# Scaling of a head half's outputs, moved from the step of their squares into the step after it

## The chip, the cores and the metric

The kernel runs on one core of one Trainium2 chip. The metric is the device time of one execution in microseconds (us). It is one layer of a gated mixer block over 2048 tokens of width 1024, in float32 with matrix products split into a high and a low part.

## What is computed

The reference, cut to the part that the change touches (the other branch, the norms at both ends and the output projection are left out):

```python
def _hgrn2_chunk_step(state, inp):          # scan over chunks of 64 tokens, per head
    ...
    o = o_inter + jnp.einsum('bhts,bhsv->bhtv', scores, v)
    ...

def reference(x, c, w_ada, ...):
    h = rms_norm(x, g_pre[l]) * (1.0 + scale) + shift
    (pv, pg, hq, hf, hi, hg, mg_pool, mg_hgrn) = jnp.split(h @ w_in[l], split_idx, axis=-1)
    ...
    o = hgrn2(q, k, v, logf)                                   # 8 heads of 128
    o = rms_norm(o, hgrn_norm_g[l]).astype(x.dtype).reshape(b, s, HGRN_WIDTH)
    branch_b = (o * jax.nn.silu(hg)) @ w_hgrn_o[l]
    merged = jax.nn.sigmoid(mg_pool) * branch_a + jax.nn.sigmoid(mg_hgrn) * branch_b
    y = merged @ w_out[l]
    x = x + gate * rms_norm(y, g_post[l])
```

The change is in the `rms_norm(o, ...)` of each head: the mean of the squares of a token's 128 outputs, its power -1/2, and the product of the outputs with it.

## The kernel before

The 2048 tokens are worked through in two passes of 1024 (`p` 0 and 1), and a pass in two halves of 512 tokens (`t` 0 and 1). A pass has these stages: the value projection for all heads (`v_job`); a loop over the 8 heads; the pool branch's output projection (`a_job`, accumulators psA), the recurrent branch's output projection and the merge (`b_job`, psB), and the last projection (`y_job`, psy). Pass 0 loads raw weights from memory, splits each on ScalarE (a cast, L172) and VectorE (a subtraction, L172) into a tile `whl` and stores the split tiles; pass 1 loads the split tiles back.

In the head loop three projections are made for a head by `quad`: "fq", and then "m" and "gp" (head 7 has "gp" first). A quad makes seven products of 12 matmuls each by a Strassen-like scheme, in four PSUM banks pa, pb, pe and pd. The sixth product (into pe) and the seventh (into pd) matter here: pd is first filled by ScalarE with a copy of pa, `A.copy(d, a)` at L496 (in the profile `pdm<-pam` or `pdgp<-pagp`), and TensorE then adds the seventh product to it. So TensorE can't begin the seventh product before that copy is done. The copy reads what the fifth product left in pa, so it could run while TensorE makes the sixth.

Between the products, `quad` calls `tick()`, which advances every active generator by one step (up to its next `yield`). The recurrence of a head is such a generator, `hgrn(p, h, t, cx)`, two of them per head, one for each half `t`; they are advanced one after the other in the same tick. They start after the head's "fq" quad and end in the next head's middle quad. Their last steps are: the output matmuls `po` (one PSUM bank of four 128x128 blocks), then four Squares on ScalarE (L687, `junk`), each with its sum into a column of `ss`; two small instructions on GpSimd (POOL in the profile) that turn the sums into the factor (L688 and the power, L390, 128x4); four scalings on ScalarE (L692, `on<-po,ss`); later four transposes on TensorE (L698, `pot<-ident,on`), and VectorE's product with norm gain and gate (L700, `sgg`), which is split into Gh and Gl for the stage psB. The outputs of heads 0 to 6 are scaled while the next head's middle quad runs ("m"; in head 7 "gp"), just ahead of its copy at L496; those of head 7 during `a_job`.

The order of the instructions within a step is not that of the code alone: the framework's scheduler merges the steps and the quad's own work into one order for each engine, and each engine then works strictly in that order, waiting on semaphores. What shares ScalarE's order with the scalings is the quad's copies, the weight casts, and the next head's score preparation (copies L605, L608, L638 into tiles `X8` and `X32`, and L709, a copy of 16 columns for the pool branch).

Of the kernel before, what the change touches and what calls it, by code (L numbers as in the profile page):

```python
# [69 lines left out]
def tile_block(ctx: ExitStack, tc: tile.TileContext, x, c, w_ada, b_ada, g_pre, g_post, w_in,  # L70
# [20 lines left out]
    def utile(name, dt=F32):  # L91
        return up.tile([P, T], dt, tag="u", name=name)
# [296 lines left out]
    def tt(o, a, b, op=MUL, e=None):  # L389
        return (e or V).tensor_tensor(o, a, b, op=op)  # L390
# [131 lines left out]
    def hgrn(p, h, t, cx):  # L522
# [164 lines left out]
            A.activation(junk[:, 0:P], po[:, cc, :], AF.Square, accum_out=ss[:, cc:cc + 1])  # L687
        G.tensor_scalar(ss, ss, 1.0 / P, EPS, op0=MUL, op1=ADD)  # L688
        tt(ss, ss, mh[:, 0:NT], op=ALU.pow, e=G)
        on = utile("on" + n)  # L690
        for cc in range(NT):
            A.activation(on[:, cc * P:(cc + 1) * P], po[:, cc, :], AF.Copy, scale=ss[:, cc:cc + 1])  # L692
        yield
        yield
        yield
        pot = px.tile([P, T], F32, tag="px", name="pot" + n)
# [308 lines left out]
    for p in range(NPASS):  # L1005
# [34 lines left out]
        for h in range(NH):  # L1040
# [22 lines left out]

            quad("fq" + n, cx, fq, tick)
            active.extend(hgrn(p, h, t, cx) for t in range(2))
            tick()
            for i, kind in enumerate(KINDS[h == NH - 1]):
# [67 lines left out]
```

## Time and profile before

| | |
|---|---|
| median of 3 runs | 1851.86 us (1851.43, 1851.86, 1857.75) |
| profiled execution, its own time | 1851.48 us |
| its span in the profile | 1849.7 us |
| granted TensorE clock, mean of the span | 0.997 of full speed |
| TensorE busy (PE) | 1782.6 us, 96% |
| weight loads (PEld) | 1456.7 us, 79% |
| VectorE busy (DVE) | 1089.1 us, 59% |
| ScalarE busy (ACT) | 799.9 us, 43% |
| GpSimd busy (POOL) | 80.0 us, 4% |

The span is the time from the first to the last recorded instruction; the execution's own time is 1.8 us more. A share is an average over all stages. In rows of instructions the time is counted from the span's start, and what stands in brackets is how long the engine sat idle before the instruction and what ended that wait.

### The profile page before, as it was taken

The page shows a single profiled execution, that of the slowest core. Times are in us where ns is not written, and L with a number is a line of the kernel's source. Part 1 is how long each engine was busy: PE and PEld are TensorE (multiplying, and loading weights), DVE is VectorE, ACT ScalarE, POOL GpSimd, SP SyncE. Part 2 cuts the span into 40 slices and gives each one's busy share as a digit, 9 for nine tenths or more (in the row PEclk, how much of TensorE's full clock was granted, in tenths as well). Part 3 has the DMA queues.
Part 4 walks back from the last instruction along what each step waited for, and adds up shares of the span by engine and source line. Part 5 has one row for each costly group of instructions (what it writes and reads, how often), then busy time and mean ns, then how long its engine had stood idle before and what let it go on. Part 6 is the DMA issues. An engine that isn't in the chain of part 4 may idle for free.

```text
span 1849.7 us, 31713 instructions
## 1 busy us (share of the span) xinstructions
PE 1782.6 (96%) x12053; PEld 1456.7 (79%) x12053; DVE 1089.1 (59%) x2328; ACT 799.9 (43%) x1863; POOL 80.0 (4%) x136
## 2 busy tenths in 40 slices
PE   5999999999999999999999999999999999999997
PEld 4788878878888777787788778878888788788886
DVE  7568877887888884565432255465455456533322
ACT  4746656656556562223322335445344344311111
POOL 1100000000000000000000000000000000000000
PEclk9999999999999999999999999999999999999999
DMA  8697676676767759987887765664764764694476
GB/s 298 233 322 277 221 268 243 231 261 225 266 241 246 247 201 320 361 288 255 295 310 242 246 193 175 224 206 154 234 205 159 231 201 162 233 340 163 141 258 230
DMA packets 236530, 444.19 MB, mean 240 GB/s; under 512 B 18989, under 2 KB 109786, under 8 KB 236378
## 3 DMA queue, kind: packets, MB, share of 16 engines
q1 hardware_dynamic: 236378, 442.17, 69.9%
q8 instruction: 95, 1.56, 0.3%
q14 instruction: 57, 0.47, 0.1%
HBM read 269.61 MB, written 172.49 MB: 239 GB/s over the span
## 4 chain that ended last, share of the span: by engine, by line
PE 79%; ACT 6%; DMA 3%; DVE 3%; POOL 2%; issue 2%; SPq 1%; POOLq 0%; DVEq 0%; ACTq 0%
PE psB L278 9%; PE psV L278 8%; PE psy L278 8%; PE pafq L278 6%; PE pagp L278 6%; PE pam L278 5%; PE pefq L278 5%; PE psA L278 4%; PE pegp L278 4%; PE pem L278 3%; PE psa L278 3%; PE pbfq L278 2%; PE pbm L278 2%; PE pdfq L278 2%; PE pdm L278 2%; PE pbgp L278 2%
## 5 line engine op out<-in xcount | busy, mean ns | idle before, releaser
L172 DVE TENSOR_TENSOR whl<-wr,whl 128x512 fp32r<-128x512 f32 x210 | 143.7, 689 | 83.6 <-ACT whl L172 82.6
L172 ACT CAST whl<-wr 128x512 fp32r<-128x512 f32 x210 | 129.8, 620 | 128.6 <-DMA wr<-in_w_hgrn_o_dram 22.4
L278 PE MATMUL psy<-whl,mgh 128*128 128x512 f32 x512 | 160.1, 393 | 1.4 <-DVE y L390 0.7
L278 PE MATMUL psV<-whl,hB 128*128 128x512 f32 x512 | 161.3, 397 | 0.1
L278 PE MATMUL psB<-Gh,whl 128*128 128x512 f32 x512 | 158.6, 390 | 0.0
L578 DVE COPY_PREDICATED PT<-mask,psa 128x256 f32<-128x256 uint8 x160 | 86.1, 548 | 51.5 <-PE psa L278 51.5
L278 PEld LDWEIGHTS psy<-whl,mgh 128*128 128x128 f32 x512 | 95.0, 188 | 22.5 <-DMA whl<-scr_y 1.7
L278 PEld LDWEIGHTS psB<-Gh,whl 128*128 128x128 f32 x512 | 96.1, 188 | 20.5 <-issue 0.5
L278 PEld LDWEIGHTS psV<-whl,hB 128*128 128x128 f32 x512 | 96.6, 191 | 19.8 <-ACT V L787 0.3
L278 PE MATMUL psV<-whl,lB 128*128 128x512 f32 x256 | 100.8, 395 | 0.0
L278 PE MATMUL psB<-Gl,whl 128*128 128x512 f32 x256 | 100.0, 391 | 0.0
L278 PE MATMUL psy<-whl,mgl 128*128 128x512 f32 x256 | 100.0, 391 | 0.0
L278 PE MATMUL pam<-hT,whl 128*128 128x512 f32 x256 | 87.2, 402 | 0.0
L278 PE MATMUL pagp<-hT,whl 128*128 128x512 f32 x256 | 86.1, 397 | 0.0
L278 PE MATMUL psA<-Ph,whl 128*128 128x512 f32 x256 | 82.6, 397 | 3.4 <-DVE sm L390 1.7
L278 PE MATMUL pafq<-hT,whl 128*128 128x512 f32 x256 | 84.0, 389 | 0.0
L390 DVE TENSOR_TENSOR K<-K,TT 128x256 f32<-128x256 f32 x192 | 81.2, 424 | 1.0 <-PE psa L278 0.9
L278 PEld LDWEIGHTS psa<-X,K 128*32 128x32 f32 x2816 | 50.1, 110 | 29.8 <-issue 21.1
L172 ACT CAST mgh<-sm 128x512 fp32r<-128x512 f32 x32 | 19.7, 620 | 121.3 <-DVE sm L390 121.3
L390 DVE TENSOR_TENSOR y<-psy,gg 128x512 f32<-128x512 f32 x32 | 21.9, 688 | 73.9 <-ACT jy L893 73.7
L278 PE MATMUL psa<-X,K 128*32 128x48 f32 (+2 forms) x2816 | 61.0, 208 | 2.1 <-DVE PT L572 2.1
L572 DVE COPY_PREDICATED PT<-mask,psa 128x256 f32<-128x256 uint8 (+1 forms) x96 | 51.9, 541 | 18.3 <-PE psa L278 18.3
(358 smaller groups left out, 4307.5 us busy)
## 6 DMA issues: line engine op xcount, KB each, us to landing
wr<-in_w_in_dram SPq DMA_DIRECT2D x122, 256.0 KB, 4.4
whl<-scr_y SPq DMA_DIRECT2D x48, 512.0 KB, 4.4
sm<-Sd SPq DMA_DIRECT2D x64, 256.0 KB, 4.3
whl<-scr_v SPq DMA_DIRECT2D x32, 512.0 KB, 3.4
wa<-in_w_ada_dram SPq DMA_DIRECT2D x32, 256.0 KB, 5.4
x<-in_x_dram SPq DMA_DIRECT2D x32, 256.0 KB, 5.5
Vd<-V SPq DMA_DIRECT2D x32, 256.0 KB, 2.4
scr_v<-whl SPq DMA_DIRECT2D x16, 512.0 KB, 2.8
```

Source lines behind the costliest of these rows:

```text
L172: return A.copy(hi, src32), V.tensor_tensor(lo, src32, hi.bitcast(F32), op=SUB)
L278: PE.matmul(o, lhsT=l, rhs=r, start=start, stop=stop, skip_group_check=True)
L390: return (e or V).tensor_tensor(o, a, b, op=op)
L572: V.copy_predicated(dst.rearrange("p (c a) b -> p c a b", c=NT), m.unsqueeze(1).broadcast_to(shp), src.unsqueeze(2).broadcast_to(shp))
L578: V.copy_predicated(dst.rearrange("p (c q) a b -> p c q a b", c=NT), m, src.rearrange("p c (a b) -> p c a b", b=b).unsqueeze(2) .broadcast ...
```

## The change

One `yield` moves up by a few lines, ahead of the scalings; the number of steps stays the same. The scalings (L692 before, L693 after) now belong to the step after the Squares, and both halves' Squares are made in the tick before.

```diff
             A.activation(junk[:, 0:P], po[:, cc, :], AF.Square, accum_out=ss[:, cc:cc + 1])
         G.tensor_scalar(ss, ss, 1.0 / P, EPS, op0=MUL, op1=ADD)
         tt(ss, ss, mh[:, 0:NT], op=ALU.pow, e=G)
+        yield
         on = utile("on" + n)
         for cc in range(NT):
             A.activation(on[:, cc * P:(cc + 1) * P], po[:, cc, :], AF.Copy, scale=ss[:, cc:cc + 1])
-        yield
         yield
         yield
         pot = px.tile([P, T], F32, tag="px", name="pot" + n)
```

No instruction is added or removed; the scheduler puts some in another place. In the names below the numbers after a tile's name are pass, head and half, and a buffer number.

The first place is ScalarE in pass 0 during head 1's "m" quad, where head 0's outputs are scaled, up to the copy at L496 (`pdm`). Before:

```order
L687 ACTIVATE junk0_0_0_1_2461,ss0_0_1_2460<-po0_0_1_2450 128x128
L692 ACTIVATE on0_0_0_2445<-po0_0_0_2424,ss0_0_0_2434 128x128 x4
L687 ACTIVATE junk1_0_0_1_2463,ss0_0_1_2460<-po0_0_1_2450 128x128
L608 COPY X8_0_1_0_2686<-sq0_1_0_2273 128x16x16
L687 ACTIVATE junk2_0_0_1_2465,ss0_0_1_2460<-po0_0_1_2450 128x128
L605 COPY X8_0_1_1_2713<-sq0_1_1_2186 128x16x16
L687 ACTIVATE junk3_0_0_1_2467,ss0_0_1_2460<-po0_0_1_2450 128x128
L692 ACTIVATE on0_0_1_2471<-po0_0_1_2450,ss0_0_1_2460 128x128 x4
L496 COPY pdm0_1_2526<-pam0_1_2304 128x512
```

Now:

```order
L687 ACTIVATE junk0_0_0_1_2456,ss0_0_1_2455<-po0_0_1_2445 128x128
L693 ACTIVATE on0_0_0_2546<-po0_0_0_2424,ss0_0_0_2434 128x128
L687 ACTIVATE junk1_0_0_1_2458,ss0_0_1_2455<-po0_0_1_2445 128x128
L693 ACTIVATE on0_0_0_2546<-po0_0_0_2424,ss0_0_0_2434 128x128
L687 ACTIVATE junk2_0_0_1_2460,ss0_0_1_2455<-po0_0_1_2445 128x128
L693 ACTIVATE on0_0_0_2546<-po0_0_0_2424,ss0_0_0_2434 128x128
L687 ACTIVATE junk3_0_0_1_2462,ss0_0_1_2455<-po0_0_1_2445 128x128
L693 ACTIVATE on0_0_0_2546<-po0_0_0_2424,ss0_0_0_2434 128x128
L608 COPY X8_0_1_0_2686<-sq0_1_0_2273 128x16x16
L693 ACTIVATE on0_0_1_2551<-po0_0_1_2445,ss0_0_1_2455 128x128 x4
L605 COPY X8_0_1_1_2713<-sq0_1_1_2186 128x16x16
L496 COPY pdm0_1_2516<-pam0_1_2304 128x512
```

The four scalings of half 0 are now dealt out between the Squares of half 1, and the two copies into X8, which stood between those Squares, stand behind them; one of them is now behind the scalings of half 1. The copy `pdm` still comes last. Heads 2 to 6 of pass 0 read the same way, with the L709 copy also moved behind half 1's scalings in heads 2, 4 and 6. In pass 1 all four scalings of half 0 alternate with all four Squares of half 1; L605 stands just ahead of half 1's scalings, and behind them come L638 and L608 in heads 1, 3 and 5 (before: L638 between the Squares, L608 behind `pdm`), L709 and L608 in heads 2, 4 and 6 (before: L709 between the Squares, L608 where it is now).

The second place is ScalarE in pass 0 during head 7's "gp" quad, where head 6's outputs are scaled. Before:

```order
L687 ACTIVATE junk0_0_6_1_7534,ss0_6_1_7533<-po0_6_1_7523 128x128
L692 ACTIVATE on0_6_0_7518<-po0_6_0_7497,ss0_6_0_7507 128x128 x4
L687 ACTIVATE junk1_0_6_1_7536,ss0_6_1_7533<-po0_6_1_7523 128x128
L605 COPY X8_0_7_1_7793<-sq0_7_1_7254 128x16x16
L687 ACTIVATE junk2_0_6_1_7538,ss0_6_1_7533<-po0_6_1_7523 128x128
L687 ACTIVATE junk3_0_6_1_7540,ss0_6_1_7533<-po0_6_1_7523 128x128
L692 ACTIVATE on0_6_1_7544<-po0_6_1_7523,ss0_6_1_7533 128x128 x4
L496 COPY pdgp0_7_7599<-pagp0_7_7372 128x512
L172 CAST whl194_7632<-wr193s1_7630 128x512
L608 COPY X8_0_7_0_7766<-sq0_7_0_7341 128x16x16
L750 ACTIVATE sgg0_7_1_7627<-c22gp0_7_7411 128x512
```

Now:

```order
L687 ACTIVATE junk0_0_6_1_7529,ss0_6_1_7528<-po0_6_1_7518 128x128
L605 COPY X8_0_7_1_7793<-sq0_7_1_7254 128x16x16
L687 ACTIVATE junk1_0_6_1_7531,ss0_6_1_7528<-po0_6_1_7518 128x128
L687 ACTIVATE junk2_0_6_1_7533,ss0_6_1_7528<-po0_6_1_7518 128x128
L687 ACTIVATE junk3_0_6_1_7535,ss0_6_1_7528<-po0_6_1_7518 128x128
L496 COPY pdgp0_7_7589<-pagp0_7_7372 128x512
L172 CAST whl194_7632<-wr193s1_7630 128x512
L608 COPY X8_0_7_0_7766<-sq0_7_0_7341 128x16x16
L750 ACTIVATE sgg0_7_1_7617<-c22gp0_7_7411 128x512
L693 ACTIVATE on0_6_0_7620<-po0_6_0_7497,ss0_6_0_7507 128x128 x4
L693 ACTIVATE on0_6_1_7625<-po0_6_1_7518,ss0_6_1_7528 128x128 x4
```

Here both scalings move behind the copy `pdgp` and the three instructions that follow it. In pass 1 head 7's "gp" quad reads the same, with L638 between the Squares and L608 ahead of `pdgp`.

The third place is TensorE in `a_job` of pass 0, where head 7's scaled outputs are transposed (pot). Before:

```order
L278 MATMUL psA0_6_0_8418<-Ph0_3_0_7493,whl206_8196 128x512
L698 MATMUL pot0_7_0_8432<-ident_87,on0_7_0_8321 128x128 x4
L278 MATMUL psA0_6_1_8452<-Ph0_0_1_7842,whl206_8196 128x512
L278 MATMUL psA0_6_1_8452<-Pl0_0_1_7843,whl206_8196 128x512
L278 MATMUL psA0_6_1_8452<-Ph0_0_1_7842,whl206_8196 128x512
L698 MATMUL pot0_7_1_8442<-ident_87,on0_7_1_8347 128x128 x4
L278 MATMUL psA0_6_1_8452<-Ph0_1_1_7874,whl206_8196 128x512
```

Now:

```order
L278 MATMUL psA0_7_0_8485<-Pl0_3_0_7494,whl207_8263 128x512
L698 MATMUL pot0_7_0_8432<-ident_87,on0_7_0_8375 128x128 x4
L278 MATMUL psA0_7_0_8485<-Ph0_3_0_7493,whl207_8263 128x512
L278 MATMUL psA0_7_1_8499<-Ph0_0_1_7842,whl207_8263 128x512
L278 MATMUL psA0_7_1_8499<-Pl0_0_1_7843,whl207_8263 128x512
L698 MATMUL pot0_7_1_8442<-ident_87,on0_7_1_8380 128x128 x4
L278 MATMUL psA0_7_1_8499<-Ph0_0_1_7842,whl207_8263 128x512
```

Both groups of transposes now stand 23 matmuls later, in the next accumulator pair. In pass 1 they move by 7 and 10 matmuls, within the same pair. On ScalarE, head 7's eight Squares now all come ahead of its eight scalings, in both passes. GpSimd's order is unchanged; SyncE's and VectorE's change by a few neighbouring rows around these places.

## Rows read from the trace of the kernel before

**Rows 1.** The head of the profile's page: the span, and each engine's busy time in us (share of the span) and instructions.

```profile
span 1849.7 us, 31713 instructions
PE 1782.6 (96%) x12053; PEld 1456.7 (79%) x12053; DVE 1089.1 (59%) x2328; ACT 799.9 (43%) x1863; POOL 80.0 (4%) x136
```

**Rows 2.** Who waited for whom, TensorE alone: engine, tile and line that waited, what it waited for, us in total, times, longest.

```profile
PE pdm L278 <- ACT pdm L496: 14.4, 12, 1.3
...
PE pdgp L278 <- ACT pdgp L496: 3.2, 2, 2.1
PE pot L698 <- ACT on L692: 2.2, 1, 2.2
```

**Rows 3.** The same for ScalarE: its wait for GpSimd's factor.

```profile
ACT on L692 <- POOL ss L390: 47.3, 32, 2.2
```

**Rows 4.** TensorE in order of time: start, duration, the instruction, and in brackets its idle time before it. The first matmul of the seventh product in pass 0's head 1, in pass 0's head 7 and pass 1's head 7, and the second group of head 7's transposes in pass 0.

```profile
239.89 0.50 PE L278 MATMUL pdm<-hT,whl 128*128 128x512 f32 x1 [1.24 <-ACT pdm L496]
...
677.83 0.50 PE L278 MATMUL pdgp<-hT,whl 128*128 128x512 f32 x1 [2.15 <-ACT pdgp L496]
...
755.33 0.66 PE L698 MATMUL pot<-ident,on 128*128 128x128 f32 x4 [2.19 <-ACT on L692]
...
1583.24 0.50 PE L278 MATMUL pdgp<-hT,whl 128*128 128x512 f32 x1 [1.06 <-ACT pdgp L496]
```

**Rows 5.** ScalarE in order of time in pass 0's head 1, from the scalings of head 0's half 0 to the copy pdm.

```profile
234.06 1.14 ACT L692 ACTIVATE on<-po,ss 128x128 f32<-128x128 f32 x4 [1.41 <-POOL ss L390]
235.07 0.29 ACT L687 ACTIVATE junk<-po 128x128 bf16<-128x128 f32 x1
...
235.32 0.43 ACT L608 COPY X<-sq 128x256 f32<-128x256 f32 x1
235.62 0.31 ACT L687 ACTIVATE junk<-po 128x128 bf16<-128x128 f32 x1
...
235.88 0.44 ACT L605 COPY X<-sq 128x256 f32<-128x256 f32 x1
236.17 0.32 ACT L687 ACTIVATE junk<-po 128x128 bf16<-128x128 f32 x1
236.34 0.24 ACT L687 ACTIVATION_READ_ACCUMULATOR junk<-po 128x1 f32 x1
238.20 1.14 ACT L692 ACTIVATE on<-po,ss 128x128 f32<-128x128 f32 x4 [1.62 <-POOL ss L390]
239.22 0.61 ACT L496 COPY pdm<-pam 128x512 f32<-128x512 f32 x1
```

**Rows 6.** ScalarE at the same place in pass 0's head 2.

```profile
306.81 1.15 ACT L692 ACTIVATE on<-po,ss 128x128 f32<-128x128 f32 x4 [1.41 <-POOL ss L390]
...
309.10 0.25 ACT L687 ACTIVATION_READ_ACCUMULATOR junk<-po 128x1 f32 x1
309.19 0.25 ACT L709 COPY PV<-halo 128x16 f32<-128x16 f32 x1
310.98 1.14 ACT L692 ACTIVATE on<-po,ss 128x128 f32<-128x128 f32 x4 [1.54 <-POOL ss L390]
312.00 0.61 ACT L496 COPY pdm<-pam 128x512 f32<-128x512 f32 x1
```

**Rows 7.** ScalarE at the same place in pass 1's head 1.

```profile
1142.54 1.14 ACT L692 ACTIVATE on<-po,ss 128x128 f32<-128x128 f32 x4 [1.42 <-POOL ss L390]
...
1145.28 0.19 ACT L687 ACTIVATION_READ_ACCUMULATOR junk<-po 128x1 f32 x1
1147.17 1.14 ACT L692 ACTIVATE on<-po,ss 128x128 f32<-128x128 f32 x4 [1.70 <-POOL ss L390]
1148.18 0.61 ACT L496 COPY pdm<-pam 128x512 f32<-128x512 f32 x1
```

**Rows 8.** ScalarE at the same place in pass 1's head 2.

```profile
1213.97 1.14 ACT L692 ACTIVATE on<-po,ss 128x128 f32<-128x128 f32 x4 [1.41 <-POOL ss L390]
...
1216.55 0.19 ACT L687 ACTIVATION_READ_ACCUMULATOR junk<-po 128x1 f32 x1
1218.34 1.15 ACT L692 ACTIVATE on<-po,ss 128x128 f32<-128x128 f32 x4 [1.60 <-POOL ss L390]
...
1219.66 0.61 ACT L496 COPY pdm<-pam 128x512 f32<-128x512 f32 x1
```

**Rows 9.** GpSimd in order of time: the first of the pair of instructions that make the factor, for half 0 and half 1 of head 0 and for half 1 of head 6, all in pass 0.

```profile
232.33 0.53 POOL L688 TENSOR_SCALAR ss<-ss 128x4 f32<-128x4 f32 x1 [32.03 <-ACT junk L687]
...
236.68 0.22 POOL L688 TENSOR_SCALAR ss<-ss 128x4 f32<-128x4 f32 x1 [2.65 <-ACT junk L687]
...
674.03 0.99 POOL L688 TENSOR_SCALAR ss<-ss 128x4 f32<-128x4 f32 x1 [2.49 <-ACT junk L687]
```

**Rows 10.** VectorE in order of time: what it ran when the first and the third of these ran (a sum or difference of two 128x512 tiles).

```profile
232.13 0.68 DVE L239 TENSOR_TENSOR wr<-wr67s,wr 128x512 f32<-128x512 f32 x1
...
674.29 0.67 DVE L239 TENSOR_TENSOR wr<-wr193s,wr 128x512 f32<-128x512 f32 x1
```

**Rows 11.** TensorE in order of time: the last matmul of the fifth product (into pagp) in pass 0's head 7.

```profile
672.58 0.39 PE L278 MATMUL pagp<-hT,whl 128*128 128x512 f32 x1
```

**Rows 12.** Busy time by stretch: us, then busy us (instructions) of PE, PEld, DVE, ACT and POOL, granted clock, share of the DMA engines, GB/s. The stretch of a_job in pass 0, and that of psB behind it.

```profile
710.00:763.00 53.00, 48.11 (x271) 40.05 (x265) 20.90 (x39) 14.89 (x48) 3.28 (x6) 1.00 0.97 345
763.00:850.00 87.00, 87.00 (x382) 71.28 (x381) 53.24 (x81) 18.50 (x31) 0.41 (x2) 1.00 0.83 287
```

## The prediction

> **What bounds the kernel now.** I read the page's head first: TensorE is busy 96% of the span, ScalarE 43%, GpSimd 4% [rows 1]. So an edit on ScalarE pays only where TensorE stands still for it. The view of who waited for whom, for TensorE alone, says where: 12 times for the copy pdm (14.4 us), twice for the copy pdgp (3.2 us), once for head 7's scalings (2.2 us) [rows 2]. That is 19.8 us, all that this edit can remove from TensorE directly. The same view for ScalarE says what makes those copies late: ScalarE waited 32 times for GpSimd's factor, 47.3 us in all, 1.5 us each [rows 3]. The timelines show the order of events: scalings of half 0, three Squares of half 1, a wait of 1.62 us for the factor, scalings of half 1, and only then the copy at L496 [rows 5], for which TensorE has by then waited [rows 4].
>
> **What the change does to each place.** No instruction is added or removed, so only waits and order can pay. I take the time t0 at which half 0's first scaling starts as fixed, since everything ahead of it is as before (in pass 1 one Square moves, dealt with below), and ask when the copy at L496 starts.
>
> Pitches from rows: four scalings take 1.01 us until the next Square starts, 0.25 each; a Square followed by other work takes 0.25, a copy into X8 0.30; a Square's start to the end of its readout is 0.41 (236.17 to 236.58); four scalings until the copy is 1.02 [rows 5].
>
> Pass 0, heads 1, 3, 5. Before: last readout ends at t0+2.52, the second scaling starts 1.62 later, pdm at t0+5.16 [rows 5]. Now three scalings and two Squares precede the last Square: 3 x 0.25 + 2 x 0.25 = 1.26, readout ends at 1.67. With the same 1.62 the scalings start at 3.29, and 1.02 + 0.30 for the one X8 copy now behind them puts pdm at 4.61: 0.55 us earlier. The fourth scaling and the other X8 copy (0.55) fit into the 1.62 of waiting, so they cost nothing; without that wait they would cost themselves.
>
> Pass 0, heads 2, 4, 6. Before: readout ends at t0+2.54, pdm at 5.19, and the wait from readout to scaling is 1.63 [rows 6]. Now 1.67 + 1.63 + 1.02 + 0.30 and some 0.2 for the L709 copy, which also moved behind: 4.82, 0.37 earlier.
>
> Pass 1, heads 1, 3, 5. Before: readout at t0+2.93, wait 1.70, pdm at 5.64 [rows 7]. Now four scalings and three Squares precede: 4 x 0.25 + 3 x 0.25 + 0.41 = 2.17; then 1.70 + 1.02, and two X copies (0.60) that now stand ahead of pdm: 5.49, 0.15 earlier. L608 waits for a VectorE step behind L605; L605 ends more than 2 us before L608's turn, so I count no wait.
>
> Pass 1, heads 2, 4, 6. Before: readout 2.77, wait 1.60, pdm 5.69 [rows 8]. Now 2.17 + 1.60 + 1.02 + 0.30 + 0.2 = 5.29, 0.40 earlier.
>
> Each of these gains is smaller than the wait it cuts into (1.24 in the row, 1.2 on average) [rows 2, 4], so it counts in full: 3 x (0.55 + 0.37 + 0.15 + 0.40) = 4.4 us.
>
> Head 7's "gp" quad. Both scalings leave the way of pdgp altogether. The copy can start when the fifth product ends, about 672.97 in pass 0 [rows 11], and takes 0.6; TensorE needs it at 677.83 - 2.15 = 675.68. So the full waits of 2.15 and 1.06 go [rows 4]. What is late next: the scalings wait for VectorE's sum behind pdgp, but their transposes come only after the seventh product, 2.7 us on. 3.2 us.
>
> Head 7's transposes in pass 0. They waited 2.19 us [rows 4]. At 0.23 us a matmul, 23 matmuls further on is 5.3 us after the place they should have had (753.14), that is 758.4, when the scalings, which ended before 755.33 even in the old order, have long been done. 2.19 us. The outputs reach psB later by 3 us, which needs them only with the last quarter of its first 48 matmuls, over 7 us after it starts; I count nothing. Pass 1 had no wait there and gets none.
>
> Sum: 4.4 + 3.2 + 2.2 = 9.8 us.
>
> **GpSimd against VectorE.** The 1.62 us are not a constant. GpSimd's first instruction takes 0.22 us in one row, 0.53 and 0.99 in others [rows 9], and both long ones ran beside a VectorE addition of two 128x512 tiles [rows 10]. The half 1 pair now starts 0.85 us sooner in pass 0, when VectorE is still at the previous scores. Its bounds are 0.22, as now (nothing lost), and 0.53, the nearest long row (0.31 lost in each of six heads, 1.9 us). VectorE's step there is half as long as that addition and partly reads PSUM, so I stay near the lower bound: 0.1 each, 0.6 us.
>
> The Trainium skill ("GPSIMD Engine Reference", section 1, Specifications) has GpSimd share its SBUF interfaces with VectorE, with contention when VectorE reads two SBUF inputs. The trace agrees, with the 0.53 and 0.99 above; by the rule alone, taken at 0.53, the sum would be 7.9, and without it 9.8.
>
> So the forecast is 9.2 us off the profiled execution's own time of 1851.48 (its span and 1.8 us around it): 1842.3. The median of the runs is 0.38 above that execution, so **1842.7** on the median's scale, 0.5% below it. About 0.5%, 9.3 us, is what a measurement of this kernel can tell from no change, so the forecast lies on the bound.
>
> **Rivals.**
>
> *The gain is waited out in a_job.* There the DMA engines are 0.97 busy at 345 GB/s and TensorE 48.11 of 53 us [rows 12]. If transfers set the pace there, what pass 0 gained before it (3 x 0.92 + 2.15 - 0.6 = 4.3) and the transposes' 2.19 come back as waits for tiles. Left: 9.2 - 6.5 = 2.7, or 1849.2. For it: that share. Against: those loads are issued as earlier work releases them, so they start earlier too, and psB behind it is busy 87.00 of 87 us [rows 12], with no sign of starving.
>
> *GpSimd's factor takes its long time everywhere.* At 0.99 in place of 0.22, 0.77 more in each of twelve heads 1 to 6: 9.2 us, of which 0.6 are already counted. Left: about 0.6, or 1851.2. Against: the one long row is from head 7's quad; the long one of head 0 is 0.53 [rows 9]. (It is what the rule above would give at its worst.)
>
> *Scalings and Squares don't overlap* (slower). No row shows a scaling that starts right behind a Square. If each waited for the other's end, a scaling would be 1.14 - 3 x 0.25 = 0.38 and a Square with its readout 0.41 [rows 5], 0.83 a pair with two small gaps, in place of 0.5 to 0.55. For a pair cost c the twelve heads together gain 3 x [(2.52 - 3c - 0.30) + (2.54 - 3c - 0.5) + (2.93 - 4c - 0.60) + (2.77 - 4c - 0.2)] = 27.5 - 42c, and 5.4 us come from head 7. At c = 0.83 that is 2.0 us slower than now, or 1853.9; it decides from c = 0.78. Against: a Square behind a scaling and a copy behind a Square each start 0.25 after it [rows 5].
>
> *More than counted.* ScalarE's casts and VectorE's sums behind L496 also come earlier, and the remaining waits at pdm, 0.7 to 1.0 us each, could shrink where something I took as fixed moves too: 12 us or more off, below 1840.
>
> That the change doesn't do what it says is excluded by the order of instructions: the moves stand there.
>
> **Chances.** The forecast, 7 to 12 us off (1839.9 to 1844.9): 0.62. Waited out in a_job: 0.16. GpSimd long: 0.08. No overlap: 0.07. More: 0.07. Of the forecast's 0.62 some 0.37 lies beyond 9.3 us, which with the last case makes 0.44 for faster; the rest of the forecast, the two middle rivals and most of the slower one are within 0.5%: 0.52; 0.04 for slower, where a pair costs still more than I priced. The range, 1839.5 to 1850.5, takes in the forecast, the a_job rival and the better half of GpSimd's; the slower case and the large gain stay out.
>
> **What would show it.** Right: TensorE's waits for pdm fall from 14.4 to about 10 us, those for pdgp and for head 7's scalings go; ScalarE's waits for the factor shrink from 47.3 to some 30; half 1's last readout ends about 1.7 us after half 0's first scaling in pass 0 and 2.2 in pass 1. Wrong: Squares among the scalings 0.4 us apart or more; GpSimd's first instruction over 0.5 us in many heads; new waits of TensorE in a_job (for psA or pk) that add up to what was removed; or a wait of L608 ahead of pdm in pass 1.

## The result: 12.4 to 13.5 us faster

| | before | after |
|---|---|---|
| median in the same comparison | 1853.35 us (4 runs, 1851.43 to 1857.75) | 1839.86 us (4 runs, 1839.0 to 1840.88) |
| profiled execution, its own time | 1851.48 us | 1839.0 us |
| its span | 1849.7 us | 1837.1 us |

The ratio is 0.9925, with a 95% interval of 0.991 to 0.994; on a second occasion it was 0.9933 (0.992 to 0.9947). That is 0.7% faster, 12.4 to 13.5 us by the medians and 12.5 from profile to profile. I had forecast 9.2, and had given "within 0.5%" a larger chance than "faster". The direction and the places were right, and the gain was a third larger than forecast.

The head of the page after, against [rows 1]:

```profile
span 1837.1 us, 31719 instructions
PE 1783.4 (97%) x12053; PEld 1457.3 (79%) x12053; DVE 1090.8 (59%) x2328; ACT 799.2 (44%) x1863; POOL 77.9 (4%) x136
```

The same work is done in less time, as it should be where only order changes. Who waited for whom, TensorE first, then ScalarE's wait for the factor, against [rows 2, 3]:

```profile
PE psa L332 <- DVE acc L325: 13.4, 4, 9.5
PE pdm L278 <- ACT pdm L496: 8.0, 12, 0.9
...
PE psA L278 <- DMA Ph<-Pd: 2.3, 3, 0.9
...
PE psA L278 <- DVE sm L390: 1.2, 2, 0.9
...
ACT on L693 <- POOL ss L390: 30.9, 26, 1.4
```

The waits for pdgp and for head 7's transposes have no row any more; pdm fell from 14.4 to 8.0. Together 11.8 us of TensorE's waits went. In a_job nothing came back: the waits for psA sum to 3.5 us above, and were 3.7:

```profile
PE psA L278 <- DVE sm L390: 1.7, 2, 1.5
PE psA L278 <- DMA Ph<-Pd: 1.7, 2, 1.2
...
PE psA L278 <- DMA Pl<-Pd: 0.3, 1, 0.3
```

ScalarE in pass 0's head 1 after, from half 0's first scaling to the copy pdm (start, duration, instruction, idle time before it), against [rows 5]:

```profile
235.38 0.37 ACT L693 ACTIVATE on<-po,ss 128x128 f32<-128x128 f32 x1 [1.42 <-POOL ss L390]
235.64 0.27 ACT L687 ACTIVATE junk<-po 128x128 bf16<-128x128 f32 x1
...
236.14 0.29 ACT L687 ACTIVATE junk<-po 128x128 bf16<-128x128 f32 x1
...
236.64 0.30 ACT L687 ACTIVATE junk<-po 128x128 bf16<-128x128 f32 x1
236.80 0.24 ACT L687 ACTIVATION_READ_ACCUMULATOR junk<-po 128x1 f32 x1
...
238.45 1.14 ACT L693 ACTIVATE on<-po,ss 128x128 f32<-128x128 f32 x4 [0.86 <-POOL ss L390]
239.47 0.42 ACT L605 COPY X<-sq 128x256 f32<-128x256 f32 x1
239.76 0.61 ACT L496 COPY pdm<-pam 128x512 f32<-128x512 f32 x1
```

Squares and scalings do overlap: a pair takes 0.50 us, so the slower rival is out. The last readout ends at 237.04, 1.66 after the first scaling (forecast 1.67). But the scalings of half 1 start 1.41 us after that, not 1.62, and pdm at 4.38 after the first scaling, not 4.61.

What GpSimd and VectorE ran there, first after, then before. The power (L390) began beside a predicated copy after, and beside a product of two SBUF tiles before:

```profile
237.13 0.20 POOL L688 TENSOR_SCALAR ss<-ss 128x4 f32<-128x4 f32 x1 [1.78 <-ACT junk L687]
237.41 1.01 POOL L390 TENSOR_TENSOR ss<-ss,mh 128x4 f32<-128x4 f32 x1
...
236.85 0.74 DVE L578 COPY_PREDICATED PT<-mask,psa 128x256 f32<-128x256 uint8 x1
237.62 0.42 DVE L390 TENSOR_TENSOR sq<-X,TT 128x256 f32<-128x256 f32 x1
```

```profile
236.98 1.19 POOL L390 TENSOR_TENSOR ss<-ss,mh 128x4 f32<-128x4 f32 x1
...
236.43 0.41 DVE L390 TENSOR_TENSOR sq<-sq,TT 128x256 f32<-128x256 f32 x1
236.87 0.43 DVE L390 TENSOR_TENSOR X<-sq,TT 128x256 f32<-128x256 f32 x1
```

In all six heads of pass 0 the power took 1.18 to 1.19 us before and 1.01 after. A product of two SBUF tiles ran beside the power after, too, but it began 0.21 us later than the power (237.62), and neither was longer for it: 1.01 and 0.42 us.

### The profile page after: what moved, and what is told of

Read it like the earlier page. It is cut to its first block, busy times and chain, and to the rows that moved or that the text cites. A ratio compares the mean times of both kernels' runs of the same rounds, so it can differ in the third digit from the quotient of the medians.

```text
span 1837.1 us, 31719 instructions
## 1 busy us (share of the span) xinstructions
PE 1783.4 (97%) x12053; PEld 1457.3 (79%) x12053; DVE 1090.8 (59%) x2328; ACT 799.2 (44%) x1863; POOL 77.9 (4%) x136
## 4 chain that ended last, share of the span: by engine, by line
PE 80%; ACT 5%; DMA 4%; DVE 3%; POOL 2%; issue 2%; SPq 1%; POOLq 0%; DVEq 0%; ACTq 0%
PE psB L278 9%; PE psV L278 8%; PE psy L278 7%; PE pafq L278 7%; PE pagp L278 6%; PE pam L278 5%; PE pefq L278 5%; PE psA L278 4%; PE pegp L278 4%; PE pem L278 3%; PE psa L278 3%; PE pbfq L278 2%; PE pbm L278 2%; PE pdfq L278 2%; PE pdm L278 2%; PE pbgp L278 2%
## 5 line engine op out<-in xcount | busy, mean ns | idle before, releaser
L390 DVE TENSOR_TENSOR K<-K,TT 128x256 f32<-128x256 f32 x192 | 81.3, 424 | 1.3 <-PE psa L278 1.2
L390 DVE TENSOR_TENSOR y<-psy,gg 128x512 f32<-128x512 f32 x32 | 21.9, 688 | 74.4 <-ACT jy L893 74.3
```

## The experiments

Theory A: what is gained is what TensorE waited for the copy at L496 and for head 7's transposes, place by place, and the rest of the 12.5 us has causes of its own to be found. Its rivals are in the expectations.

### How much does an unchanged kernel vary?

The kernel before, again.

> The kernel before, unchanged, profiled a second time: how much the small waits of TensorE move from one execution to another. A: its sum of waits for pdm, pdgp and pot is 19.8 us again within 0.3, and the other waits differ by up to 1 us in the sum, which would be enough for the 0.8 us of the difference that no wait moved by the change holds. B (those 0.8 us are the change's): the other waits repeat within 0.3 us in the sum. Ratio 1.000 within 0.001.

1852.55 us, ratio 1.0002 (0.9994 to 1.0011), span 1849.4. The waits for pdm, pdgp and pot are 14.4, 3.2 and 2.2 us again, to the tenth. TensorE's other waits, without the first load's, sum to 29.5 us in place of 31.3: they move by 1.8, nearly twice what I allowed. So no cause can be read out of one microsecond of small waits.

This trace shows something that the first trace of the same kernel does not. Busy time by stretch (columns as in [rows 12]), first of this run from 752 to 759 us, then of the changed kernel in the same 7 us:

```profile
752.00:759.00 7.00, 5.42 (x19) 4.51 (x20) 2.40 (x4) 2.27 (x6) 0.35 (x1) 0.76 1.04 398
```

```profile
752.00:759.00 7.00, 7.00 (x34) 5.84 (x33) 4.49 (x8) 1.86 (x3) 0.00 (x0) 1.00 0.88 332
```

The granted clock is 0.76 of full speed over these 7 us, so it was at its lower level (1.2 GHz) for about half of them; what stood ahead of the fall is the wait of 2.17 us of head 7's transposes:

```profile
753.58 1.12 PE L698 MATMUL pot<-ident,on 128*128 128x128 f32 x4 [2.17 <-ACT on L692]
```

0.24 x 7 = 1.7 us of full-speed work are lost. The trace that I predicted from had the same wait and no fall.

### The move in heads 0 to 5, and in heads 6 and 7, by itself

Against the changed kernel:

```diff
         tt(ss, ss, mh[:, 0:NT], op=ALU.pow, e=G)
-        yield
+        if h < 6:
+            yield
         on = utile("on" + n)
...
+        if not (h < 6):
+            yield
         yield
         yield
         pot = px.tile([P, T], F32, tag="px", name="pot" + n)
```

> The move made for the outputs of heads 0 to 5 alone (they are scaled in the middle quads of heads 1 to 6); heads 6 and 7 as before. A, the theory (each place gives what its own wait of TensorE lost, the sum is additive): the twelve waits for pdm fall from 14.4 to 8.0 us and nothing else goes, so 6.4 us off the kernel before, up to 7.2 with the small waits elsewhere: ratio 0.9961 to 0.9966; pdgp 3.2 and pot 2.2 stay. B, the rival (head 7 carries most of it, and what heads 1 to 6 save is waited out later): under 3 us off, ratio over 0.998.

1847.34 us, ratio 0.9972 (0.9963 to 0.9981): 4.8 us off. The waits for pdm are 7.9 us and those for pdgp and pot are as before, so the place is right. A's 6.4 us lie inside the interval (3.5 to 6.9 us), near its end; rival B (under 3) is out. The profiled execution was the slowest of its runs (1851.1), and its clock fell twice: at the transposes' wait of 2.17 us as above, and behind a wait of 2.54 us for a Sigmoid tile, again 1.7 us lost (0.28 x 6):

```profile
718.43 0.50 PE L278 MATMUL psA<-Ph,whl 128*128 128x512 f32 x1 [2.54 <-DVE sm L390]
```

```profile
719.00:725.00 6.00, 6.00 (x21) 4.75 (x20) 1.37 (x2) 0.00 (x0) 0.00 (x0) 0.72 0.97 323
```

That is not the whole of why it was slow: the fastest run of this kernel, 1843.95 us, has the same mean granted clock, 0.995.

The next kernel has `h >= 6` in place of `h < 6`.

> The move made for heads 6 and 7 alone (head 7's gp quad and a_job); heads 0 to 5 as before. A: pdgp 3.2 and pot 2.2 go, pdm stays at 14.4: 5.4 us off, up to 6.2, ratio 0.9967 to 0.9971. With the run of heads 0 to 5 it adds up to what the whole change gives (12 to 14 us). B (head 7 carries most): 9 us or more off, ratio under 0.995.

1844.51 us, ratio 0.996 (0.9948 to 0.9973): 7.7 us off, 5.0 to 9.6 by the interval. pdm stays at 14.4, pdgp and pot go. With the other half it adds up to 12.5 us, as expected. The two waits are 5.4 us, inside the interval, and so is B's 9: this run does not decide between them. If head 7 gives back more than the trace called waiting, 0.7 us of it are explained by the account of breaks below; that falls of the clock in the kernel before are the rest was my guess, and is not shown. Its five runs also lie close together (1843.8 to 1845.9) where the eleven of heads 0 to 5 alone go from 1843.95 to 1851.1.

### Head 6 alone, and head 7 alone

The condition is `h == 6`, then `h == 7`. A's sum has a further term here, 0.27 us for each wait that goes altogether; the rows for it stand below, under the version with no factor ahead of the copy.

> The move made for the outputs of head 6 alone (scaled in head 7's gp quad). The two waits at pdgp go, 3.2 us. A (a wait that goes altogether gives back its gap and 0.27 us more, in which TensorE refills behind it): 3.2 + 2 x 0.27 = 3.7 us off the kernel before. D (the wait of 2.2 us of head 7's transposes, which stays here, is what lets the granted clock fall in some executions of a_job): the runs lie as far apart as those of the kernel before, 5 us or more from the lowest to the highest. B, the rival (the falls of the clock come by chance, or from the waits at pdgp): they lie within 2.5 us, as those of the run with heads 6 and 7 did.

1848.15 us, ratio 0.9979 (0.997 to 0.9988): 3.9 us off, 2.2 to 5.6 by the interval, and A's 3.7 lie in it. The runs go from 1846.05 to 1852.59.

> The move made for the outputs of head 7 alone (scaled and transposed in a_job). Head 7's wait of 2.2 us goes. A: 2.2 + 0.27 = 2.5 us off in an execution without a fall of the clock. D (that wait lets the clock fall in some executions, at some 1.7 us each): the runs lie within 2.5 us of each other, and the median is 3 to 4.5 us below the kernel before, more than the wait. B (falls by chance or from pdgp): 2.5 us at the median, and the runs 5 us or more apart.

1851.2 us, ratio 0.9992 (0.9983 to 1.0001): 0.9 off, at most 3.1 by the interval, and the runs still go from 1848.25 to 1854.26. So D, which blamed the transposes' wait alone, falls; the 2.5 us of A and B lie inside the interval. Head 6 alone and head 7 alone add up to 4.8 us where both together gave 7.7; the intervals are wide enough for that, but here the sum is not shown. The profile shows the clock falling at the other place, behind the wait at pdgp that this kernel keeps:

```profile
680.50 0.78 PE L278 MATMUL pdgp<-hT,whl 128*128 128x512 f32 x1 [2.14 <-ACT pdgp L496]
```

```profile
680.00:684.00 4.00, 3.50 (x8) 2.80 (x9) 3.52 (x7) 2.98 (x6) 0.00 (x0) 0.57 0.35 121
```

0.43 x 4 is again 1.7 us. So either wait of some 2.2 us can be followed by a fall, in some executions.

> The changed kernel, unchanged, on another occasion. D2, the theory as the runs of heads 6 and of head 7 alone left it (the granted clock falls in some executions behind either of head 7's two waits of some 2.2 us in pass 0, at pdgp and at the transposes, and the change takes both away): its runs lie within 3 us of each other and those of the kernel before 5 us or more apart; no fall of the clock between 640 and 800 us of its profile; the median is 12 to 13.5 us below. B (falls by chance): its runs lie as far apart as those of the kernel before.

1839.32 us. The five runs go from 1837.3 to 1841.32 and the nine of the kernel before from 1848.37 to 1854.51: narrower, though not the 3 us I wrote down. Its profile shows no fall between 640 and 800 us. Of the five profiles with one or both waits (two of the kernel before, heads 0 to 5, head 6, head 7) three show a fall behind such a wait; the six with neither show none there, one of them (the longer factor, below) with a wait of 2.2 us for a Sigmoid tile. That is a shown place and price, but how often it happens is not settled.

The falls do not explain the spread of the runs, either. One of them is 1.7 of 1850 us, 0.001 of the mean granted clock, which every run has on record to three digits. Of the 23 runs of the kernel before that stand beside head 6 alone and head 7 alone, the eight at 0.997 go from 1849.74 to 1855.04 us and the six at 0.995 from 1849.06 to 1856.49. So D2 is not shown as the cause of the spread. Part of the difference from trace to trace lies ahead of the head loop, whose first matmul (pafq) starts between 130.24 and 133.96 us in the traces: each shows a fall of the clock there as well, and in those of head 6 alone and head 7 alone it costs 3.4 us in place of 1.7 or 1.8 (granted 0.87 from 38 to 64 us; 0.93 in the two of the kernel before).

### No factor ahead of the copy

The changed kernel, with ScalarE's scalings ordered behind the quad's copy in all heads:

```diff
-        A.copy(d, a)
+        last["pd"] = A.copy(d, a)
...
-        for cc in range(NT):
-            A.activation(on[:, cc * P:(cc + 1) * P], po[:, cc, :], AF.Copy, scale=ss[:, cc:cc + 1])
+        with after(last["pd"]):
+            for cc in range(NT):
+                A.activation(on[:, cc * P:(cc + 1) * P], po[:, cc, :], AF.Copy, scale=ss[:, cc:cc + 1])
```

> The changed kernel with one thing more: ScalarE's scalings are ordered behind the quad's copy at L496 in every head, so no factor of GpSimd stands between the Squares and that copy. A (the time gained is what TensorE waits for that copy, and nothing else stands behind it): the remaining 8.0 us at pdm go too, 1831 to 1833 us, ratio to the kernel before 0.988 to 0.989. B (what is gained in pass 0 is waited out in a_job, where the transfers are 0.97 busy): pass 1's 4.9 us alone, 1835. C (the scalings behind the copy make the transposes or the Sigmoids late, a new wait of TensorE): 1838 or more.

1825.73 us, ratio to the kernel before 0.9856 (0.9843 to 0.9869): 26 us off, and 14 us better than the change. The rivals are out, and A's 8.0 us are too few. The view of waits has no row for pdm:

```profile
PE psa L332 <- DVE acc L325: 14.3, 4, 9.1
PE xT L444 <- DVE x L416: 5.2, 5, 1.5
PE pst L139 <- DMA rows<-in_hgrn_norm_g_dram: 4.6, 1, 4.6
```

Where the rest is, three traces of TensorE show: the last matmul of the sixth product and the first two of the seventh in pass 0's head 1. First of this kernel, then of the change, then the rows of the kernel before that stand around the first row of [rows 4]:

```profile
239.13 0.39 PE L278 MATMUL pem<-hB,whl 128*128 128x512 f32 x1
239.35 0.39 PE L278 MATMUL pdm<-hT,whl 128*128 128x512 f32 x1
239.58 0.39 PE L278 MATMUL pdm<-lT,whl 128*128 128x512 f32 x1
```

```profile
239.58 0.39 PE L278 MATMUL pem<-hB,whl 128*128 128x512 f32 x1
240.43 0.50 PE L278 MATMUL pdm<-hT,whl 128*128 128x512 f32 x1 [0.46 <-ACT pdm L496]
240.76 0.40 PE L278 MATMUL pdm<-lT,whl 128*128 128x512 f32 x1
```

```profile
238.26 0.39 PE L278 MATMUL pem<-hB,whl 128*128 128x512 f32 x1
...
240.22 0.40 PE L278 MATMUL pdm<-lT,whl 128*128 128x512 f32 x1
```

From the first to the last of the three it takes 0.45 us without a wait, 1.18 with one of 0.46, and 1.96 with one of 1.24. Less the wait, a break costs 0.27 us in both: a matmul counts as busy for 0.39 while the next one starts 0.22 behind it, so a wait's first 0.17 us pass as work, and the matmul behind it is followed 0.10 later than usual. What TensorE does in that time the rows do not show. **The idle time in brackets is 0.27 us less than what the break costs, at 0.46 us as at 1.24.** That part is paid until the wait is gone altogether. That gives 8.0 + 12 x 0.27 = 11.2 of the 14 us here. TensorE's busy time shows it too: 1777.2 us for the same matmuls, 6.2 less than in the change, 3.2 of them by this account. The other 2.8 of the 14 us I can't place; the small waits vary by 1.8 between two traces of one kernel.

### A longer factor

```diff
         tt(ss, ss, mh[:, 0:NT], op=ALU.pow, e=G)
+        G.tensor_copy(ss, ss)
         yield
```

> The changed kernel with one more GpSimd instruction of 128x4 (a copy, some 0.19 us with 0.09 of gap) behind the power in each factor; computes the same. A (in heads 1 to 6 GpSimd's factors of both halves stand one after the other ahead of the copy at L496, and TensorE waits for that copy): each head's wait at pdm grows by 2 x 0.28, 12 heads 6.7 us; 1845 to 1847 us, waits for pdm 13 to 15 us, none at pdgp. B (other work of ScalarE hides the factor): 1840 to 1841, pdm as now, 8.0.

1842.06 us, 2.2 above the change (the waits for pdm grow by 2.1, to 10.1). Both figures were missed: A's 1845 to 1847 and B's 1840 to 1841. The two passes differ. In pass 0 each head's wait grows by nearly the 0.56 us that A says: head 1's from 0.46 to 0.94, head 2's from 0.60 to 1.10. In pass 1 they shrink by 0.14. There ScalarE makes half 1's first Square before it waits, in an order that the longer factor led the scheduler to, and the power took 1.01 us in place of 1.26. So A is near where the order stays, and wrong as a sum: here the added instruction also changed the order.

### GpSimd beside VectorE

Behind the changed kernel's end, GpSimd runs eight TENSOR_SCALAR and four powers of 128x4 in each of five stretches, and VectorE 18 of one kind beside them in the last four (`za`, `zb`, `zc`, `zs` and the mask `zm` are in SBUF, `zp` in PSUM):

```diff
+    kinds = [None, lambda: tt(zc, zc, zb), lambda: tt(zc, zp, zb), lambda: V.tensor_copy(zc, zb),
+             lambda: V.copy_predicated(zc, zm, zp)]
+    for kind in kinds:
...
+        for _ in range(8):
+            G.tensor_scalar(zs, zs, 1.0 / P, EPS, op0=MUL, op1=ADD)
+        for _ in range(4):
+            tt(zs, zs, mh[:, 0:NT], op=ALU.pow, e=G)
```

> The changed kernel with five stretches behind its end, in which GpSimd runs eight TENSOR_SCALAR and four powers of 128x4 each: alone, beside VectorE's products of two 128x512 tiles in SBUF, beside products of a PSUM and an SBUF tile, beside SBUF copies, and beside predicated copies from PSUM. A (VectorE's steps that read two SBUF tiles hold GpSimd up until they end): alone and beside the others 0.19 and 1.01 us; beside the two SBUF tiles 0.5 us and more for the first kind, 1.2 and more for the second. B (length comes from something else, such as GpSimd's own gaps between instructions): the five stretches are alike within 0.05 us.

GpSimd in order of time; the row of eight and the row of four of each stretch, in the order of the expectation. The number behind the x is how many instructions a row holds:

```profile
1833.97 2.12 POOL L1130 TENSOR_SCALAR zs<-zs 128x4 f32<-128x4 f32 x8 [1.04 <-DVE zs L1121]
1836.17 4.28 POOL L390 TENSOR_TENSOR zs<-zs,mh 128x4 f32<-128x4 f32 x4
...
1840.94 5.77 POOL L1130 TENSOR_SCALAR zs<-zs 128x4 f32<-128x4 f32 x8 [0.49 <-DVE zc L1134]
1846.80 5.82 POOL L390 TENSOR_TENSOR zs<-zs,mh 128x4 f32<-128x4 f32 x4
...
1854.49 2.12 POOL L1130 TENSOR_SCALAR zs<-zs 128x4 f32<-128x4 f32 x8 [1.87 <-DVE zc L1134]
1856.69 4.26 POOL L390 TENSOR_TENSOR zs<-zs,mh 128x4 f32<-128x4 f32 x4
...
1868.01 3.65 POOL L1130 TENSOR_SCALAR zs<-zs 128x4 f32<-128x4 f32 x8 [7.06 <-DVE zc L1134]
1871.75 5.34 POOL L390 TENSOR_TENSOR zs<-zs,mh 128x4 f32<-128x4 f32 x4
...
1877.58 2.12 POOL L1130 TENSOR_SCALAR zs<-zs 128x4 f32<-128x4 f32 x8 [0.49 <-DVE zc L1134]
1879.79 4.26 POOL L390 TENSOR_TENSOR zs<-zs,mh 128x4 f32<-128x4 f32 x4
```

VectorE beside the second stretch and beside the third:

```profile
1840.89 13.04 DVE L390 TENSOR_TENSOR zc<-zc,zb 128x512 f32<-128x512 f32 x18
...
1854.44 13.02 DVE L390 TENSOR_TENSOR zc<-zp,zb 128x512 f32<-128x512 f32 x18
```

Alone, a TENSOR_SCALAR comes every 0.27 us and a power every 1.07. Beside products of two SBUF tiles they come every 0.72 and 1.46. VectorE's 18 products took 13.04 us there, 0.72 each: GpSimd got through one TENSOR_SCALAR for each of VectorE's products. VectorE itself was not held up: beside GpSimd at its full rate the 18 took 13.02. Beside a product with one PSUM tile and beside predicated copies from PSUM they run as if alone. So B is out. A missed one kind: plain copies from SBUF to SBUF hold GpSimd up as well (0.46 and 1.34).

The Trainium skill ("SBUF — State Buffer", section "SBUF: two separate sides") calls the port pair that VectorE and GpSimd share an exclusive lock, held for the whole instruction. The 0.72 us beside instructions of 0.72 agree. The result's rows after do not: a product of two SBUF tiles began 0.21 us into a power, and neither waited for the other. The Trainium skill lets a VectorE instruction take that lock with two SBUF inputs or in a 2-port mode; the copies' mode itself no run here shows.

## Why the prediction was partly right

| place | forecast, us | measured, us |
|---|---|---|
| pass 0, heads 1, 3, 5, each | 0.55 | 0.79 |
| pass 0, heads 2, 4, 6, each | 0.37 | 0.71 |
| pass 1, heads 1, 3, 5, each | 0.15 | 0.20 |
| pass 1, heads 2, 4, 6, each | 0.40 | 0.44 |
| deduction for GpSimd | -0.6 | none |
| these twelve heads | 3.8 | 6.4 |
| pdgp | 3.2 | 3.2 + 0.5 |
| head 7's transposes, pass 0 | 2.2 | 2.2 + 0.2 |
| sum | 9.2 | 12.5 |

Measured are the differences of the bracketed waits; the terms behind a plus are what the breaks that went cost beside their gap (for pdgp, 675.30 to 678.17 became 671.36 to 671.81: 2.42 us for a wait of 2.15). The sum meets the 12.5 us from profile to profile, but part of that is luck: the head loop began 1.4 us later in the trace after. From its first matmul to the span's end it is 1718.8 us before and 1704.8 after (1704.9 in the change's second profile), 14.0 less. So 12.5 of 14.0 us are accounted for, and the rest I can't place; small waits alone moved by 1.8 between the two traces of the kernel before.

**Which idle time counts** held: only TensorE's waits, and only at these places. **The order of events** held to the hundredth where it depends on ScalarE alone: 1.66 for 1.67, a pair at 0.50. **Head 7** held: both scalings left the way of pdgp, and the transposes no longer wait.

**The step that failed** is the paragraph on GpSimd against VectorE, and with it the 1.62 us that each chain carried over. I asked only whether the earlier pair would be slower, and deducted 0.6. But the 1.62 of [rows 5] was itself a slowed wait: its power took 1.19 beside X<-sq. In its new place it begins beside a predicated copy from PSUM (0.74 us, not the half of an addition that I took) and takes 1.01, and the wait is 1.41. The last experiment shows that, back to back, the one kind of VectorE step holds GpSimd up and the other does not. In pass 0 this gives each head some 0.2 us, and the deduction was not due: nearly 2 of the missing 2.6 us of the twelve heads. The rest is small pieces, such as the L709 copy of heads 2, 4 and 6, counted at 0.2 and started 0.1 ahead of the next. In pass 1 the power did begin beside a product of SBUF tiles (1.26), the wait stayed near what I had taken, and the forecast is 0.05 off:

```profile
1135.56 1.26 POOL L390 TENSOR_TENSOR ss<-ss,mh 128x4 f32<-128x4 f32 x1
...
1135.52 0.42 DVE L390 TENSOR_TENSOR sq<-sq,TT 128x256 f32<-128x256 f32 x1
```

**A term that was missing**: 0.2 to 0.27 us for each wait that goes altogether, 0.7 us here, and 3.2 in the version with the scalings behind the copy.

**A cost that was not priced**: falls of the clock behind the two waits of 2.2 us. The trace I worked from has none in that stretch, so from profile to profile they add nothing; at 1.7 us each they can be in the medians, which differ by up to a microsecond more than the profiles do, but no run shows how much of that is theirs.

**The rivals.** The gain was not waited out in a_job: psA's waits stayed at 3.5 us, and the better version brought 14 us more through the same stretch. GpSimd's factor was not long everywhere, and Squares and scalings overlap. "More than counted", at 0.07, came nearest, for another reason than the one I gave: not ScalarE's later work, but GpSimd's factor. The change's time, 1839.86, lies at the low end of the range, and that too is luck: the range was worked out from a kernel before of 1851.86 us, and in this comparison it took 1853.35. By the ratio, 0.9925 of 1851.86 is 1838.0, below the range. I had put the forecast on the 0.5% bound; with the wait read as slowed it would have lain beyond.

## What to carry to other kernels

Before a wait is carried over into a new order, ask whether it is a bare one or already a slowed one: what the other engines ran during it may not be there in its new place. A stall of TensorE cost its gap and some 0.27 us more here, so taking one away altogether is worth more than shortening two by as much in all, and the best order tried here put the whole chain behind the copy that TensorE needs (1825.7 us). Where a stall is 2 us long, look at the granted clock behind it in more than one execution.

## What was not expected of the hardware

- GpSimd's TENSOR_SCALAR of 128x4 takes 0.27 us from one to the next alone, 0.72 beside VectorE's products of two SBUF tiles and 0.46 beside its SBUF copies, and is not slowed beside products and predicated copies that read PSUM.
- TensorE lost 0.27 us more than the gap at a break of 0.46 us as at one of 1.24 or 2.15.
- The granted clock fell to its lower level behind single waits of 2.14 to 2.54 us in an otherwise busy TensorE, at about 1.7 us of lost work each, in some executions and not in others: not behind those of 2.15 and 2.19 in the first trace of the kernel before.
